# A decoder layer's down projection: from eight column blocks to seven products of halves

## The chip, the cores and the metric

One core of a Trainium2 chip runs the whole layer in one launch. The metric is the device time of one execution in microseconds; smaller is better.

## The reference, cut to what matters

Batch 1, 512 tokens, width 1024, float32. The layer computes `x = x + mixers(norm(x))` and then a gated feed-forward block with a causal depthwise convolution of width 3, and a last norm:

```python
def conv_gated_ffn(h, w_up, conv_w, conv_b, w_down):
    up = causal_depthwise_conv(h @ w_up, conv_w, conv_b)     # 1024 -> 2 x 2816
    gate, val = jnp.split(up, 2, axis=-1)
    return (jax.nn.silu(gate) * val) @ w_down                # 2816 -> 1024

x = x + conv_gated_ffn(rms_norm(x, ffn_norm), w_up, conv_w, conv_b, w_down)
return rms_norm(x, final_norm)
```

The change lies in the last product (512 x 2816 by 2816 x 1024), the residual after it and the last norm.

## The kernel before, in words

**Precision.** Every large product runs in three passes of a reduced float32 type. `split` and `wsplit` (L65 to L77) make a high part by a cast on ACT and a low part by a subtraction on DVE; `mm3` (L79) issues high x high, high x low and low x high into the same PSUM bank.

**Weights.** `wtile` (L56) loads a tile of up to 128 x 1024 from DRAM on SP's queue into one of three raw buffers; `wsplit` writes one of three pairs of high and low buffers. A load waits until the split of the tile three before it has read its buffer, and a split waits until the matmuls three tiles back have read theirs.

**Order.** The code is written stage by stage: input projections, attention and spatial gating, output projection (L563), up projection (L614), down projection (L641), last columns and last norm (L682). The tile framework places waits where buffers and data demand them, and each engine and each queue runs its instructions in order.

**Up stage (L590 to L626).** For each of 22 channel blocks of 128, two weight tiles (gate and value) are multiplied with the normalised activations `hH`, `hL` (8 tiles of 128 x 512 each, width by tokens), 24 matmuls of 512 columns each. `conv` (L599) scales, convolves on ACT and DVE, L623 takes the SiLU, L625 multiplies, and L626 splits the result into `aH[i]`, `aL[i]`: channels by tokens.

**Down stage (L641 to L678).** For six of the eight output blocks of 128 columns, 22 blocks of channels x 3 matmuls accumulate `pd`: width by tokens, weights stationary, 512 tokens moving. Then the residual is added (L649), squared (L651), summed into `acc3` and scaled by the gain. The last two blocks' weights `w_e` are loaded and split once, ahead (L657 to L678), into the buffers of `hH`, `hL`.

**The end (L682 to L735).** The last two column blocks are multiplied for the first 384 tokens (L689), whose norm needs sums over partitions by small matmuls (`rooted`, `over_partitions`) and whose output leaves as width by tokens. The last 128 tokens are done by token: activations stationary, 256 columns of weights moving (L705), the six finished blocks transposed on PE (L693), the mean of squares per partition.

**POOL** does a few powers (the root of the norms), a mask and memsets; it issues no DMA.

Of the kernel before, what the change touches and what calls it, by code (L numbers as in the profile page):

```python
# [42 lines left out]
def block_kernel(ctx, tc, xT, pos, w_s, w_v, w_g, w_q, w_kv, w_o, w_u, w_d,  # L43
                 ws_t, bs, vg, vb, par, cst, w_e, fnl, out, outB):
# [569 lines left out]
    for i in range(NF):  # L614
        pg = up(2 * i)
        if i == 0:
            rt = rooted([acc2], 0, f2, "f")
            pv = up(1)
            A.copy(r2, over_partitions(rt, f2, "f"))
        yg = conv(pg, i)  # L620
        if i:
            pv = up(2 * i + 1)
        A.activation(out=yg, in_=yg, func=AF.Silu)  # L623
        yv = conv(pv, NF + i)
        V.tensor_tensor(out=yv, in0=yg, in1=yv, op=ALU.mult)  # L625
        split(aH[i], aL[i], yv)  # L626

    acc3 = fp.tile([P, S], F32, name="acc3")

    def gain(j):  # L630
        return part[:, PFN + j:PFN + j + 1]

    def dweights(j):
        parts = []
        for lo, hi in ((0, 8), (8, 15), (15, 22)):
            n = (hi - lo) * P
            raw = wtile(w_d[j, :, lo * P:hi * P], f"d{j}{lo}", cols=n)
            parts.append((hi - lo,) + tuple(wsplit(raw, f"d{j}{lo}", 0, n)))
        return parts

    for j in range(KC - 2):  # L641
        pd = bank(f"pd{j}")
        i = 0
        for n, wh, wl in dweights(j):
            for a in range(n):
                c = slice(a * P, (a + 1) * P)
                mm3(pd, wh[:, c], wl[:, c], aH[i], aL[i], i == 0, i == NF - 1)
                i += 1
        V.tensor_tensor(out=x1[j], in0=pd, in1=x1[j], op=ALU.add)  # L649
        sq = acc3 if j == 0 else f2.tile([P, S], F32, tag="z", name=f"sq3_{j}")  # L650
        A.activation(out=sq, in_=x1[j], func=AF.Square)  # L651
        if j:
            V.tensor_tensor(out=acc3, in0=acc3, in1=sq, op=ALU.add)
        A.mul(x1[j], x1[j], gain(j))
        if j == 1:

            eh, el = [], []  # L657
            xh = fp.tile([P, 6 * 2 * P], F32R, name="xh")
            xl = fp.tile([P, 6 * 2 * P], F32R, name="xl")
            for q in range(6):  # L660
                lo = q * 1024
                raw = wtile(w_e[:, lo:min(lo + 1024, NF * 2 * P)], f"e{q}", cols=min(1024, NF * 2 * P - lo))
                for k in range(4):
                    i = 4 * q + k
                    if i >= NF:
                        continue
                    if i < 16:
                        if i % 2 == 0:
                            t = i // 2
                            th = hp.tile([P, S], F32R, tag=f"hH{t}", name=f"eH{t}")  # L670
                            tl = hp.tile([P, S], F32R, tag=f"hL{t}", name=f"eL{t}")
                            split(th, tl, raw[:, k * 256:k * 256 + S])
                        o = (i % 2) * 256
                    else:
                        th, tl, o = xh, xl, (i - 16) * 256
                        split(th[:, o:o + 256], tl[:, o:o + 256], raw[:, k * 256:k * 256 + 256])
                    eh.append(th[:, o:o + 256])
                    el.append(tl[:, o:o + 256])  # L678
# [3 lines left out]
    n = S - P  # L682
    tA, tB = slice(0, n), slice(n, S)
    pA, sqA = None, []
    for j in (KC - 2, KC - 1):
        pA = bank(f"pA{j}")
        for i in range(NF):
            c = slice((j - KC + 2) * P, (j - KC + 3) * P)
            mm3(pA[:, :n], eh[i][:, c], el[i][:, c], aH[i][:, tA], aL[i][:, tA], i == 0, i == NF - 1)  # L689
            if j == KC - 2 and i == 11:  # L690
                pT = [bank("pTa"), bank("pTb")]
                for k in range(KC - 2):
                    T.transpose(pT[k // 4][:, (k % 4) * P:(k % 4 + 1) * P], x1[k][:, tB], ident)  # L693
                pmB = bank("pm_B")
                col_mean(pmB[:, :1], [acc3[:, tB]], 0)
                mB = fp.tile([P, 4], F32, name="mB")
                V.tensor_scalar(out=mB[:, 0:1], in0=pmB[:, 0:1], scalar1=EPS, scalar2=None, op0=ALU.add)
        V.tensor_tensor(out=x1[j][:, tA], in0=pA[:, :n], in1=x1[j][:, tA], op=ALU.add)
        sq = f2.tile([P, n], F32, tag="z", name=f"sqA{j}")
        A.activation(out=sq, in_=x1[j][:, tA], func=AF.Square)  # L700
        V.tensor_tensor(out=acc3[:, tA], in0=acc3[:, tA], in1=sq, op=ALU.add)
        A.mul(x1[j][:, tA], x1[j][:, tA], gain(j))
    pB = bank("pB")
    for i in range(NF):
        mm3(pB[:, :256], aH[i][:, tB], aL[i][:, tB], eh[i], el[i], i == 0, i == NF - 1)  # L705
        if i == 1:

            for k in range(2):
                T.matmul(pB[:, k * P:(k + 1) * P], lhsT=x1[KC - 2 + k][:, tB], rhs=ident, start=False, stop=False)
        if i == 4:  # L710
            rt = rooted([acc3[:, tA]], 0, f2, "A", cols=NT - 1)
        if i == 12:
            pb = over_partitions(rt, f2, "A", cols=NT - 1)
            for q in range(KC // 2):
                for j in (2 * q, 2 * q + 1):
                    V.tensor_tensor(out=x1[j][:, tA], in0=x1[j][:, tA], in1=pb, op=ALU.mult)
                    if q in (0, 3):
                        SY.dma_start(out[j], x1[j][:, tA])
                if q in (0, 3):
                    continue  # L720
                SY.dma_start(out[2 * q:2 * q + 2].rearrange("j p t -> p j t"),
                             x1t[q].rearrange("p (j t) -> p j t", j=2)[:, :, tA])
# [92 lines left out]
```

## Time and profile before

| | us |
|---|---|
| median of 3 runs (708.59 to 710.53) | 708.83 |
| the profiled execution, its own time | 709.26 |
| its span | 707.6 |
| PE busy in it | 699.6 |
| DVE busy | 476.5 |
| ACT busy | 331.5 |
| POOL busy | 12.3 |

PE busy counts the time in which a matmul runs. A matmul's own duration overlaps that of the next one, so the pace is read from starts. "Idle before" of an engine, in brackets or behind the bar, is the time it stood still ahead of an instruction, and what ended that. DMA share is the mean busy share of the core's 16 DMA engines.

### The profile page before, as it was taken

The numbers are of one execution on the slowest core, as the hardware profiler recorded it, in microseconds if no ns is written. First come the engines' busy times: TensorE is split into PE (matmuls) and PEld (weight loads), VectorE is DVE, ScalarE is ACT, GpSimd is POOL, SyncE is SP. The second block draws the span as 40 slices with busy tenths as digits, with TensorE's granted clock in tenths as the row PEclk, the third lists the DMA queues.
The fourth block names the chain that finished last, engine by engine and source line by source line (L and its number), as shares of the span: only waits on it lengthen the run. The fifth ranks groups of instructions, "written<-read, shape, count | busy, mean of one in ns | idle before, by whom it ended". The sixth has DMA issues, their size and how long they took to land.

```text
span 707.6 us, 8629 instructions
## 1 busy us (share of the span) xinstructions
PE 699.6 (99%) x3303; PEld 586.6 (83%) x3303; DVE 476.5 (67%) x817; ACT 331.5 (47%) x496; POOL 12.3 (2%) x16
## 2 busy tenths in 40 slices
PE   9999999999999999999999999999999999999996
PEld 6888888888888888888888888888888888888896
DVE  8875799877777578755587777777677765433104
ACT  5464556676667533433454444444444444423101
POOL 0000110000000000000100000000000000000000
PEclk9999999999999999999999999999999999999999
...
GB/s 260 179 77 135 168 83 82 60 113 40 69 72 60 33 87 76 190 94 105 93 98 89 90 102 107 90 90 100 108 89 91 95 98 163 194 87 48 0 1 120
DMA packets 22617, 69.63 MB, mean 98 GB/s; under 512 B 2736, under 2 KB 4400, under 8 KB 22576
## 3 DMA queue, kind: packets, MB, share of 16 engines
q1 hardware_dynamic: 21568, 66.72, 28.9%
...
q8 instruction: 26, 0.43, 0.3%
...
## 4 chain that ended last, share of the span: by engine, by line
PE 94%; DVE 3%; DMA 2%; issue 0%; ACT 0%; SPq 0%; POOLq 0%; DVEq 0%
PE pup L81 11%; PE pup L82 11%; PE pup L80 11%; PE pd L81 4%; PE pd L80 4%; PE pd L82 4%; PE pout L81 2%; PE pout L80 2%; PE pout L82 2%; PE pzb L82 2%; PE pzb L80 2%; PE pzb L81 2%; PE pv L80 2%; PE pv L82 2%; PE pza L81 2%; PE pv L81 2%
## 5 line engine op out<-in xcount | busy, mean ns | idle before, releaser
L70 ACT CAST wh_u<-wr_u 128x1024 fp32r<-128x1024 f32 x44 | 46.3, 1052 | 41.6 <-PE pup L81 29.5
L71 DVE TENSOR_TENSOR wl_u<-wr_u,wh_u 128x1024 fp32r<-128x1024 f32 x44 | 53.9, 1226 | 8.0 <-ACT wh_u L70 7.0
L604 DVE TENSOR_TENSOR z<-pup,r 128x512 f32<-128x512 f32 x44 | 30.2, 688 | 35.1 <-PE pup L82 35.1
L80 PE MATMUL pd<-aH,wh_d 128*128 128x512 f32 x132 | 51.3, 389 | 0.0
L81 PE MATMUL pd<-aL,wh_d 128*128 128x512 f32 x132 | 51.3, 389 | 0.0
L82 PE MATMUL pd<-aH,wl_d 128*128 128x512 f32 x132 | 51.3, 389 | 0.0
L70 ACT CAST wh_g<-wr_g 128x1024 fp32r<-128x1024 f32 x24 | 25.2, 1050 | 44.4 <-issue 23.3
L76 ACT CAST aH<-y 128x512 fp32r<-128x512 f32 x22 | 13.7, 621 | 56.7 <-DVE z L603 54.2
L71 DVE TENSOR_TENSOR wl_d<-wr_d,wh_d 128x896 fp32r<-128x896 f32 (+1 forms) x18 | 20.5, 1136 | 29.0 <-ACT wh_d L70 28.6
L70 ACT CAST wh_d<-wr_d 128x896 fp32r<-128x896 f32 (+1 forms) x18 | 17.7, 982 | 43.2 <-PE pd L81 35.2
L606 ACT ACTIVATE y<-z,part 128x512 f32<-128x512 f32 x44 | 35.9, 818 | 3.4 <-DVE z L604 1.8
L71 DVE TENSOR_TENSOR wl_g<-wr_g,wh_g 128x1024 fp32r<-128x1024 f32 x24 | 29.4, 1224 | 7.0 <-ACT wh_g L70 6.9
L610 DVE SCALAR_TENSOR_TENSOR y<-z,part,y 128x512 f32<-128x512 f32 x44 | 33.0, 752 | 1.4
L608 DVE SCALAR_TENSOR_TENSOR y<-z,part,y 128x512 f32<-128x512 f32 x44 | 32.8, 747 | 0.3 <-ACT y L606 0.3
L623 ACT ACTIVATE y<-y 128x512 f32<-128x512 f32 x22 | 13.9, 632 | 36.4 <-DVE y L610 36.4
L80 PEld LDWEIGHTS pd<-aH,wh_d 128*128 128x128 f32 x132 | 24.8, 188 | 5.2
L82 PEld LDWEIGHTS pd<-aH,wl_d 128*128 128x128 f32 x132 | 24.8, 188 | 5.2
L81 PEld LDWEIGHTS pd<-aL,wh_d 128*128 128x128 f32 x132 | 24.8, 188 | 5.1
L81 PE MATMUL pout<-mL,wh_o 128*128 128x512 f32 x64 | 25.4, 397 | 0.0
L82 PE MATMUL pout<-mH,wl_o 128*128 128x512 f32 x64 | 25.3, 395 | 0.0
L80 PE MATMUL pout<-mH,wh_o 128*128 128x512 f32 x64 | 25.2, 396 | 0.0
L77 DVE TENSOR_TENSOR aL<-y,aH 128x512 fp32r<-128x512 f32 x22 | 15.2, 693 | 14.2 <-ACT aH L76 14.2
...
## 6 DMA issues: line engine op xcount, KB each, us to landing
wr_u<-in_w_u_dram SPq DMA_DIRECT2D x44, 512.0 KB, 3.3
wr_g<-in_w_g_dram SPq DMA_DIRECT2D x24, 512.0 KB, 3.3
...
wr_v<-in_w_v_dram SPq DMA_DIRECT2D x8, 512.0 KB, 4.2
wr_o<-in_w_o_dram SPq DMA_DIRECT2D x8, 512.0 KB, 3.2
wr_d<-in_w_d_dram SPq DMA_DIRECT2D x6, 512.0 KB, 3.5
wr_e<-in_w_e_dram SPq DMA_DIRECT2D x5, 512.0 KB, 3.7
```

Of the source, the lines that this page charges most:

```text
L70: A.copy(th[:, lo:hi], raw[:, lo:hi])
L71: V.tensor_tensor(out=tl[:, lo:hi], in0=raw[:, lo:hi], in1=th[:, lo:hi].bitcast(F32), op=ALU.subtract)
L76: A.copy(th, src)
L77: V.tensor_tensor(out=tl, in0=src, in1=th.bitcast(F32), op=ALU.subtract)
L80: T.matmul(o, lhsT=wh, rhs=xh, start=start, stop=False)
L81: T.matmul(o, lhsT=wh, rhs=xl, start=False, stop=False)
L82: T.matmul(o, lhsT=wl, rhs=xh, start=False, stop=stop)
L604: V.tensor_tensor(out=z[:, 2:], in0=pz, in1=r2, op=ALU.mult)
L606: A.activation(out=y, in_=z[:, 2:], func=AF.Identity, scale=part[:, w + 2:w + 3], bias=part[:, PCB + f:PCB + f + 1])
L608: V.scalar_tensor_tensor(out=y, in0=z[:, 1:S + 1], scalar=part[:, w + 1:w + 2], in1=y, op0=ALU.mult, op1=ALU.add)
L610: V.scalar_tensor_tensor(out=y, in0=z[:, 0:S], scalar=part[:, w:w + 1], in1=y, op0=ALU.mult, op1=ALU.add)
L623: A.activation(out=yg, in_=yg, func=AF.Silu)
```

## The change

The product is cut into halves in all three directions: tokens 0 to 255 and 256 to 511 (A1x, A2x), channels 0 to 1407 and 1408 to 2815 (Ax1 with B1x, Ax2 with B2x), output columns 0 to 511 and 512 to 1023. Seven products of halves take the place of eight, in Winograd's form, in the order m1, m5, m6, m4, m3, m7, m2:

| product | left | right |
|---|---|---|
| m1 | A11 | B11 |
| m5 | A21 - A22 | B11 + B12 |
| m6 | A21 - A22 - A11 | B11 + B12 + B22 |
| m4 | A22 | B11 + B12 + B21 + B22 |
| m3 | A12 + A21 - A22 - A11 | B22 |
| m7 | A11 - A21 | B12 + B22 |
| m2 | A12 | B21 |

Each product has 2 blocks of 128 tokens (stationary) by 512 columns (moving) over 11 channel blocks, cut into five steps of two blocks and one of one; a step of two is 12 matmuls.

- *Left sides.* The up stage keeps its result unsplit in `aT`, channel blocks of the two halves in turn; after every two blocks of each half `a_sides` splits A11 and forms the four sums in place on DVE. The other six left sides are split during the product before.
- *Right sides.* m1 and m2 read their weights through `wtile` on SP's queue. For the other five, six tiles `R` (which take the memory of `hH`, `hL` of the up stage, now one tile `h0` to `h7` each) are filled from POOL's queue: B11 plain, B12 added; and after each step's split the next change: + B22, + B21, B22 anew, + B12. Adding is done by the DMA (`accum_op`).
- *Residual.* It is transposed to token-major in the up stage (`x1_turn`: 32 transposes on PE, 8 copies on ACT). Parts that several outputs share are added into it by DMAs from POOL's queue (`plus`, 16 of them, 128 KB each); the rest by DVE out of PSUM (`done`).
- *The end.* All tokens are done by token: squares with their sum on ACT, root on POOL, gain and root on DVE and ACT, two stores per 128 tokens (SP and ACT). m2's last three steps run for its first token block, then for its second. `w_e`, the transposes and norm matmuls of the old end are gone; the gain is loaded for the whole width, later.

The diff, without the removed lines of the old down stage and end (they stand above, L614 to L735) and the plumbing of arguments:

```diff
@@ -161,8 +160,8 @@
     hL = [None] * KC
 
     def htiles(j, n):
-        hH[j] = hp.tile([P, S], F32R, tag=f"hH{j}", name=f"hH{j}{n}")
-        hL[j] = hp.tile([P, S], F32R, tag=f"hL{j}", name=f"hL{j}{n}")
+        t = hp.tile([P, D], F32R, tag=f"h{j}", name=f"h{j}{n}")
+        hH[j], hL[j] = t[:, :S], t[:, S:]
...
@@ -557,8 +556,8 @@
             split(mH[h], mL[h], zz)
 
 
-        x1t = [hp.tile([P, D], F32, tag=f"d{t}", name=f"x1_{t}") for t in range(NT)]
-        x1 = [x1t[j // 2][:, (j % 2) * S:(j % 2 + 1) * S] for j in range(KC)]
+        x1t = [hp.tile([P, NT, NT, P], F32, tag=f"d{t}", name=f"x1_{t}") for t in range(2)]
+        x1 = [x1t[j // NT][:, j % NT].rearrange("p t c -> p (t c)") for j in range(KC)]
         acc2 = hp.tile([P, S], F32, name="acc2")
         for j in range(KC):
             SY.dma_start(x1[j], xT[j])
...
@@ -582,10 +581,26 @@
 
 
     fp = ctx.enter_context(tc.tile_pool(name="fp", bufs=1))
-    f2 = ctx.enter_context(tc.tile_pool(name="f2", bufs=2))
     r2 = fp.tile([P, S], F32, name="r2")
-    aH = [fp.tile([P, S], F32R, name=f"aH{i}") for i in range(NF)]
-    aL = [fp.tile([P, S], F32R, name=f"aL{i}") for i in range(NF)]
+    aT = fp.tile([P, NF, S], F32, name="aT")
+    KH = NF // 2
+    S2 = S // 2
+    s1 = fp.tile([P, KH, S2], F32, name="s1")
+    s4 = fp.tile([P, KH, S2], F32, name="s4")
+    a1h = fp.tile([P, KH, S2], F32R, name="a1h")
+    a1l = fp.tile([P, KH, S2], F32R, name="a1l")
+    def a_sides(lo, hi):
+        A11, A21 = aT[:, lo:hi, :S2], aT[:, lo:hi, S2:]
+        A12, A22 = aT[:, KH + lo:KH + hi, :S2], aT[:, KH + lo:KH + hi, S2:]
+        h_, l_, s1_, s4_ = (t[:, lo:hi] for t in (a1h, a1l, s1, s4))
+        split(h_, l_, A11)
+        V.tensor_tensor(out=s1_, in0=A21, in1=A22, op=ALU.subtract)
+        V.tensor_tensor(out=A21, in0=A11, in1=A21, op=ALU.subtract)
+        V.tensor_tensor(out=A11, in0=s1_, in1=A11, op=ALU.subtract)
+        V.tensor_tensor(out=s4_, in0=A12, in1=A11, op=ALU.add)
 
     def up(f):
         raw = wtile(w_u[f], f"u{f}")
@@ -611,128 +626,195 @@
                                op0=ALU.mult, op1=ALU.add)
         return y
 
...
+    def x1_turn(t, hf):
+        pt = bank(f"pt{t}{hf}")
+        for q in range(NT):
+            T.transpose(pt[:, q * P:(q + 1) * P], x1t[hf][:, q, t, :], ident)
+        A.copy(x1t[hf][:, :, t, :], pt.rearrange("p (q c) -> p q c", q=NT))
+    with tc.tile_pool(name="f2", bufs=2) as f2:
+        for n in range(NF):
+            i = n // 2 + (n % 2) * KH
+            pg = up(2 * n)
+            if n == 0:
+                rt = rooted([acc2], 0, f2, "f")
+                pv = up(1)
+                A.copy(r2, over_partitions(rt, f2, "f"))
+            yg = conv(pg, i)
+            if n:
+                pv = up(2 * n + 1)
+            A.activation(out=yg, in_=yg, func=AF.Silu)
+            yv = conv(pv, NF + i)
+            V.tensor_tensor(out=aT[:, i], in0=yg, in1=yv, op=ALU.mult)
+            if n % 4 == 3 or n == NF - 1:
+                a_sides(n // 4 * 2, n // 2 + 1)
+            if 4 <= n < 12:
+                x1_turn((n - 4) // 2, n % 2)
+    dp = ctx.enter_context(tc.tile_pool(name="dp", bufs=1))
+    steps = [(g, min(g + 2, KH)) for g in range(0, KH, 2)]
+    NS = len(steps)
+    blocks = [(0, 4), (4, 8), (8, KH)]
+    B11, B12, B21, B22 = (w_d[k, f] for k in range(2) for f in range(2))
+    ms = fp.tile([P, NT, 4], F32, name="ms")
+    gfb = fp.tile([P, D], F32, name="gfb")
+    A.dma_start(gfb, fnl.to_broadcast([P, D]))
+    R = [hp.tile([P, D], F32, tag=f"h{g}", name=f"r1_{g}") for g in range(NS)]
+    def cols(g):
+        lo, hi = steps[g]
+        return slice(lo * S, hi * S)
+    def fill(t, q, g, add=True):
+        c = cols(g)
+        n = c.stop - c.start
+        if add:
+            G.dma_start(t[g][:, :n], q[:, c], accum_op=ALU.add)
+        else:
+            G.dma_start(t[g][:, :n], q[:, c])
+    left = {
+        "m5": lambda lo, hi: s1[:, lo:hi],
+        "m6": lambda lo, hi: aT[:, lo:hi, :S2],
+        "m4": lambda lo, hi: aT[:, KH + lo:KH + hi, S2:],
+        "m3": lambda lo, hi: s4[:, lo:hi],
+        "m7": lambda lo, hi: aT[:, lo:hi, S2:],
+        "m2": lambda lo, hi: aT[:, KH + lo:KH + hi, :S2],
+    }
+    order = ["m1", "m5", "m6", "m4", "m3", "m7", "m2"]
+    after = {"m5": (B22, True), "m6": (B21, True), "m4": (B22, False), "m3": (B12, True)}
+    parts = {}
+    def a_split(n, b):
+        lo, hi = blocks[b]
+        w = (hi - lo) * S2
+        ah = dp.tile([P, 4 * S2], F32R, tag="ah", name=f"ah_{n}{lo}", bufs=3)
+        al = dp.tile([P, 4 * S2], F32R, tag="al", name=f"al_{n}{lo}", bufs=3)
+        split(ah[:, :w].rearrange("p (k t) -> p k t", t=S2), al[:, :w].rearrange("p (k t) -> p k t", t=S2),
+              left[n](lo, hi))
+        parts[n, b] = (ah, al)
+    def a_of(n, k, m):
+        if n == "m1":
+            return tuple(t[:, k, m * P:(m + 1) * P] for t in (a1h, a1l))
+        c = slice((k % 4) * S2 + m * P, (k % 4) * S2 + (m + 1) * P)
+        return tuple(t[:, c] for t in parts[n, k // 4])
+    ws_ = {}
+    def w_split(n, g):
+        c = cols(g)
+        w = c.stop - c.start
+        if n in ("m1", "m2"):
+            raw = wtile((B11 if n == "m1" else B21)[:, c], f"{n}{g}", cols=w)
+        else:
+            raw = R[g]
+        ws_[n, g] = wsplit(raw, f"{n}{g}", 0, w)
+        if n in after:
+            fill(R, after[n][0], g, after[n][1])
+    def res(t, f):
+        return x1t[f][:, :, t, :]
+    def b3(t):
+        return t.rearrange("p (q c) -> p q c", q=NT)
+    def plus(t, f, t_):
+        for q in (slice(0, 2), slice(2, 4)):
+            G.dma_start(res(t, f)[:, q], b3(t_)[:, q], accum_op=ALU.add)
+    def done(t, f, p_, op=ALU.add):
+        V.tensor_tensor(out=res(t, f), in0=res(t, f), in1=b3(p_), op=op)
+        j_ = dp.tile([P, S], F32, tag="j", name=f"j{t}{f}", bufs=2)
+        A.activation(out=b3(j_), in_=res(t, f), func=AF.Square, accum_out=ms[:, t, f:f + 1])
+        if f:
+            V.tensor_tensor(out=res(t, f), in0=res(t, f), in1=b3(gfb[:, S:]), op=ALU.mult)
+    def finish(t):
+        V.tensor_scalar(out=ms[:, t, 2:3], in0=ms[:, t, 0:1], scalar1=ms[:, t, 1:2], scalar2=1.0 / D,
+                        op0=ALU.add, op1=ALU.mult)
+        V.tensor_scalar(out=ms[:, t, 2:3], in0=ms[:, t, 2:3], scalar1=EPS, scalar2=None, op0=ALU.add)
+        G.tensor_tensor(out=ms[:, t, 3:4], in0=ms[:, t, 2:3], in1=mhalf[:, 0:1], op=ALU.pow)
+        r_ = ms[:, t, 3:4]
+        V.scalar_tensor_tensor(out=res(t, 0), in0=res(t, 0), scalar=r_, in1=b3(gfb[:, :S]),
+                               op0=ALU.mult, op1=ALU.mult)
+        A.mul(res(t, 1), res(t, 1), r_)
+        SY.dma_start(out[t, :, :S], res(t, 0))
+        A.dma_start(out[t, :, S:], res(t, 1))
+    p1, p5 = ([fp.tile([P, S], F32, name=f"{n}{m}") for m in range(2)] for n in ("p1", "p5"))
+    def post(n, b, ms_=(0, 1)):
+        for m in ms_:
+            if n == "m1":
+                A.copy(p1[m], b[m])
+                plus(m, 0, p1[m])
+            if n == "m5":
+                A.copy(p5[m], b[m])
+            if n == "m6":
+                V.tensor_tensor(out=p1[m], in0=b[m], in1=p1[m], op=ALU.add)
+                V.tensor_tensor(out=p5[m], in0=p5[m], in1=p1[m], op=ALU.subtract)
+                plus(m, 1, p5[m])
+                plus(2 + m, 1, p5[m])
+            if n == "m4":
+                V.tensor_tensor(out=p1[m], in0=b[m], in1=p1[m], op=ALU.add)
+                plus(2 + m, 0, p1[m])
+            if n == "m3":
+                done(m, 1, b[m])
+            if n == "m7":
+                done(2 + m, 0, b[m])
+                done(2 + m, 1, b[m], ALU.subtract)
+                finish(2 + m)
+            if n == "m2":
+                with tc.high_priority():
+                    done(m, 0, b[m])
+                    finish(m)
+    seq = [(n, g) for n in order for g in range(NS)]
+    turn_ = {}
+    for i, n in enumerate(order[1:], 1):
+        for b in range(3):
+            turn_.setdefault(b if i == 1 else NS * (i - 1) + (4, 6, 8)[b], []).append((n, b))
+    for g in range(2):
+        w_split(*seq[g])
+    for g in range(NS):
+        fill(R, B11, g, False)
+    for g in range(NS):
+        fill(R, B12, g)
+    acc_ = None
+    def steps_of(n, g, ms_):
+        wh, wl = ws_[n, g]
+        lo, hi = steps[g]
+        for k in range(lo, hi):
+            cw = slice((k - lo) * S, (k - lo + 1) * S)
+            for m in ms_:
+                ah, al = a_of(n, k, m)
+                mm3(acc_[m], ah, al, wh[:, cw], wl[:, cw], k == 0, k == KH - 1)
+    for i, (n, g) in enumerate(seq):
+        if i + 2 < len(seq):
+            w_split(*seq[i + 2])
+        for x in turn_.get(i, ()):
+            a_split(*x)
+        if g == 0:
+            acc_ = [bank(f"{n}_{m}") for m in range(2)]
+        if n != order[-1] or g < NS - 3:
+            steps_of(n, g, (0, 1))
+            if g == NS - 1:
+                post(n, acc_)
+    for m in range(2):
+        for g in range(NS - 3, NS):
+            steps_of(order[-1], g, (m,))
+        post(order[-1], acc_, (m,))
 def _layout(x, positions, mix_norm, w_in, a_v_norm_g, a_v_norm_b, a_spatial_w, a_spatial_b, q_a_norm,
...
     up = cols(w_up[0])
-    a["w_u"] = c(np.stack([up[:NF], up[NF:]], axis=1).reshape(2 * NF, P, D))
-    a["w_d"] = c(cols(w_down[0][:, :D - 2 * P]))
-    a["w_e"] = c(w_down[0][:, D - 2 * P:].reshape(NF, P, 2 * P).transpose(1, 0, 2).reshape(P, NF * 2 * P))
-    a["fnl"] = c(final_norm[D - 2 * P:].reshape(1, 2 * P))
+    up = np.stack([up[:NF], up[NF:]], axis=1).reshape(2, NF // 2, 2, P, D)
+    a["w_u"] = c(up.transpose(1, 0, 2, 3, 4).reshape(2 * NF, P, D))
+    a["w_d"] = c(w_down[0].reshape(2, NF // 2, P, 2, S).transpose(0, 3, 2, 1, 4).reshape(2, 2, P, -1))
```

## Rows read from the trace of the kernel before

**Rows 1.** The page, part 1: engine, busy us, share of the span, instructions.

```profile
PE 699.6 (99%) x3303; PEld 586.6 (83%) x3303; DVE 476.5 (67%) x817; ACT 331.5 (47%) x496; POOL 12.3 (2%) x16
```

**Rows 2.** The page, part 4: the chain that ended last, by engine.

```profile
PE 94%; DVE 3%; DMA 2%; issue 0%; ACT 0%; SPq 0%; POOLq 0%; DVEq 0%
```

**Rows 3.** Timeline of PE, matmuls: start us, us, engine, line, operation.

```profile
578.10 0.39 PE L80 MATMUL pd<-aH,wh_d 128*128 128x512 f32 x1
...
649.73 0.39 PE L81 MATMUL pd<-aL,wh_d 128*128 128x512 f32 x1
...
661.97 0.39 PE L81 MATMUL pd<-aL,wh_d 128*128 128x512 f32 x1
...
674.13 0.60 PE L693 MATMUL pTa<-cstt,x 128*128 128x128 f32 x4
674.56 0.38 PE L693 MATMUL pTb<-cstt,x 128*128 128x128 f32 x2
...
689.05 0.33 PE L80 MATMUL pA<-aH,xh 128*128 128x384 f32 x1
...
691.48 0.33 PE L82 MATMUL pA<-aH,xl 128*128 128x384 f32 x1
...
694.91 0.28 PE L80 MATMUL pB<-eH,aH 128*128 128x256 f32 x1
...
696.71 0.28 PE L80 MATMUL pB<-eH,aH 128*128 128x256 f32 x1
```

**Rows 4.** Chain that ended last, in order of time: start us, us, what.

```profile
701.05 0.13 PE pB L82
```

**Rows 5.** Timeline of the end, ACT, DVE and SP's queue.

```profile
701.21 0.38 ACT L726 ACTIVATE oB<-pB 128x256 f32<-128x256 f32 x1 [4.45 <-PE pB L82]
...
701.72 0.42 DVE L727 TENSOR_TENSOR xB<-pB,gfb 128x256 f32<-128x256 f32 x1 [0.40 <-ACT oB L726]
...
703.07 0.69 ACT L731 ACTIVATE oB<-pTa,mB 128x512 f32<-128x512 f32 x1 [1.38 <-POOL mB L730]
...
703.96 0.33 SPq L735 DMA_DIRECT2D out_dram<-oB  x1
```

**Rows 6.** Groups of DVE by form, from 340 us: xcount, busy us, mean ns.

```profile
L610 DVE SCALAR_TENSOR_TENSOR y<-z,part,y 128x512 f32<-128x512 f32 x44 | 33.0, 752 | 1.4
...
L71 DVE TENSOR_TENSOR wl_d<-wr_d,wh_d 128x1024 fp32r<-128x1024 f32 x6 | 7.4, 1225 | 14.1 <-ACT wh_d L70 14.1
...
L649 DVE TENSOR_TENSOR x<-pd,x 128x512 f32<-128x512 f32 x6 | 4.1, 691 | 22.9 <-PE pd L82 22.9
```

**Rows 7.** Groups of ACT by form, from 340 us: the same columns.

```profile
L70 ACT CAST wh_d<-wr_d 128x1024 fp32r<-128x1024 f32 x6 | 6.3, 1054 | 11.6 <-PE pd L81 8.9 <-DMA wr_d<-in_w_d_dram 1.7 <-PE pup L81 1.0
...
L651 ACT ACTIVATE sq<-x 128x512 f32<-128x512 f32 x5 | 3.2, 632 | 14.1 <-DVE x L649 14.1
```

**Rows 8.** Windows: length, busy of PE, PEld, DVE, ACT, POOL; clock, DMA share, GB/s.

```profile
345.00:577.00 232.00, 232.00 (x1025) 192.06 (x1025) 171.26 (x260) 107.35 (x134) 0.94 (x1) 1.00 0.30 96
577.00:670.00 93.00, 93.00 (x415) 77.37 (x414) 35.75 (x46) 31.41 (x44) 0.00 (x0) 1.00 0.33 100
...
0.00:17.70 17.70, 16.28 (x62) 10.98 (x63) 14.36 (x32) 10.34 (x18) 1.24 (x6) 1.00 0.82 260
```

**Rows 9.** DMA: a queue's packets, MB, share; issues xcount, KB, us to landing.

```profile
q1 hardware_dynamic: 21568, 66.72, 28.9%
...
wr_u<-in_w_u_dram SPq DMA_DIRECT2D x44, 512.0 KB, 3.3
...
bsb<-in_bs_dram ACTq DMA_DIRECT2D x1, 512.0 KB, 8.2
```

**Rows 10.** Groups of POOL by form, whole span: xcount, busy us, mean ns.

```profile
L148 POOL TENSOR_TENSOR rt_f<-ms_f,mhalf 128x4 f32<-128x4 f32 x1 | 1.9, 1856 | 226.7 <-DVE ms_f L147 226.7
```

**Rows 11.** Timeline of ACT in the up stage.

```profile
480.20 1.05 ACT L70 CAST wh_u<-wr_u 128x1024 fp32r<-128x1024 f32 x1 [1.01 <-PE pup L81]
```

More of the change, by code (lines that the diff above doesn't have):

```diff
@@ L43, in block_kernel @@
 def block_kernel(ctx, tc, xT, pos, w_s, w_v, w_g, w_q, w_kv, w_o, w_u, w_d,
-                 ws_t, bs, vg, vb, par, cst, w_e, fnl, out, outB):
+                 ws_t, bs, vg, vb, par, cst, fnl, out):
     nc = tc.nc
@@ L86, in block_kernel @@
     gx = cp.tile([P, KC], F32, name="gx")
-    gfb = cp.tile([P, 2 * P], F32, name="gfb")
     cstt = cp.tile([P, NCST], F32, name="cstt")
@@ L178, in block_kernel @@
     ckL = mx.tile([P, S], F32R, name="ckL")
-    vA = [hp.tile([P, D], F32, tag=f"d{t}", name=f"vA{t}") for t in range(NT)]
+    vA2 = [hp.tile([P, 2 * D], F32, tag=f"d{t}", name=f"vA{t}") for t in range(2)]
+    vA = [vA2[t // 2][:, (t % 2) * D:(t % 2 + 1) * D] for t in range(NT)]
     with tc.tile_pool(name="st", bufs=2) as st:
@@ L612, in conv @@
         return y
[L614 to L678, printed above, removed]
@@ L682, in block_kernel @@
[L682 to L722, printed above, removed]
@@ L723, in block_kernel @@
-    oB = fp.tile([P, D], F32, name="oB")
-    xB = fp.tile([P, 2 * P], F32, name="xB")
-    with tc.high_priority():
-        A.activation(out=oB[:, S + 256:], in_=pB[:, :256], func=AF.Square, accum_out=mB[:, 1:2])
-        V.tensor_tensor(out=xB, in0=pB[:, :256], in1=gfb, op=ALU.mult)
-        V.tensor_scalar(out=mB[:, 2:3], in0=mB[:, 1:2], scalar1=1.0 / D, scalar2=mB[:, 0:1],
-                        op0=ALU.mult, op1=ALU.add)
-        G.tensor_tensor(out=mB[:, 3:4], in0=mB[:, 2:3], in1=mhalf[:, 0:1], op=ALU.pow)
-        A.mul(oB[:, :S], pT[0], mB[:, 3:4])
-        V.tensor_scalar(out=oB[:, S:S + 256], in0=pT[1][:, :256], scalar1=mB[:, 3:4], scalar2=None, op0=ALU.mult)
-        V.tensor_scalar(out=oB[:, S + 256:], in0=xB, scalar1=mB[:, 3:4], scalar2=None, op0=ALU.mult)
-        A.dma_start(outB[:, :S], oB[:, :S])
-        SY.dma_start(outB[:, S:], oB[:, S:])
+    def x1_turn(t, hf):
[3 more added lines that the diff above has]
+        A.copy(x1t[hf][:, :, t, :], pt.rearrange("p (q c) -> p q c", q=NT))
@@ L807 @@
                                    kind="ExternalInput").ap())
-    args.append(nc.dram_tensor("out_0_dram", (KC, P, S - P), F32, kind="ExternalOutput").ap())
-    args.append(nc.dram_tensor("out_1_dram", (P, D), F32, kind="ExternalOutput").ap())
+    args.append(nc.dram_tensor("out_0_dram", (NT, P, D), F32, kind="ExternalOutput").ap())
     with tile.TileContext(nc) as tc:
@@ L812 @@
     r = run_bass_kernel_spmd(nc, [maps], core_ids=[0])
-    a, b = (np.asarray(r.results[0][f"out_{i}_dram"]) for i in range(2))
-    return np.ascontiguousarray(np.concatenate([a.reshape(D, S - P).T, b]))[None]
+    return np.ascontiguousarray(np.asarray(r.results[0]["out_0_dram"]).reshape(S, D))[None]
```

4 lines of the change are left out of this document (2 added, 2 removed).

## The prediction

> **What bounds the kernel now.** I read the busy table first: PE is busy for 699.6 of 707.6 us, POOL for 12.3 [rows 1]. The chain that ended last agrees: 94% of it is PE [rows 2], so time comes off only where PE gets fewer or shorter matmuls. Then the matmul timeline gives the pace [rows 3], because a matmul's duration (0.39 us) overlaps the next one's. From 649.73 to 661.97 us lie 54 steps of 512 columns, 0.2267 us each; from 689.05 to 691.48 lie 14 of 384 columns, 0.174 each; from 694.91 to 696.71 lie 15 of 256 columns, 0.120 each. The down projection starts at 578.10 us, called T below [rows 3], and its last matmul ends at 701.18 [rows 4]: 123.1 us, with PE never idle in the window 577 to 670 and the granted clock 1.00 [rows 8]. In that window DVE works 35.8 and ACT 31.4 of 93 us: there is room on both.
>
> The profiled execution took 709.26 us (span 707.6 plus 1.7 around it), 0.43 above the median of 708.83. I sum against 709.26 and take 0.4 off at the end.
>
> **What it removes on PE.** Before: 6 column blocks x 22 x 3 = 396 matmuls of 512 columns, 132 of 384 and 66 of 256; 396 x 0.2267 + 132 x 0.174 + 66 x 0.120 = 89.8 + 23.0 + 7.9 = 120.7 us; transposes and the norms' small matmuls fill the 123.1. After: seven products, each 11 x 2 x 3 = 66 matmuls of 512 columns: 462 x 0.2267 = 104.7 us, and the norms and the token-major tail need no matmul. Gain 18.4 us. One product lasts 15.0 us, a step of 12 matmuls 2.72.
>
> **What it adds on PE.** 32 transposes in the up stage. Four took from 674.13 to 674.56, 0.11 each [rows 3]: +3.5 us, on the path, as PE has no idle time to give.
>
> **The tail.** Today 1.86 us pass from the square on ACT (701.21) to the last scaling (703.07) [rows 5]. After, a PSUM add of 0.69 (L649 [rows 6]) precedes it; the square is 512 columns wide, 0.63 (L651 [rows 7]) for 0.38, and one more small DVE operation follows; against it the product with the gain leaves the chain (0.42, L727 [rows 5]). I take +0.6 us. The last scaling, 0.75 on DVE (L610's kind [rows 6]) beside 0.69 on ACT, and two 256 KB stores are as now. The other half of m2's tokens, and all of m7's, finish under later matmuls; without that cover each would cost this tail again, some 7 us.
>
> **ACT and DVE in the down stage.** Weight splits grow from 22 to 38.5 tiles of 1024 columns, 1.05 us on ACT and 1.23 on DVE each [rows 6, 7]. Per product: DVE 5.5 x 1.23 + 5.5 x 0.69 for the left side = 10.5 us, ACT 5.5 x 1.05 + 5.5 x 0.63 = 9.2 us, of 15.0. Nothing on the path, as long as splits aren't held up by their source.
>
> **The up stage.** For each four channel blocks, four 512-column subtractions become five (one split, four sums), 0.69 us more per pair of pairs, under 4 us for the stage; DVE has 61 of 232 us free there [rows 8]. The reordered blocks cost nothing; eight ACT copies of some 0.63 us [rows 7] lie in ACT's free half [rows 8]. m1 reads only the first half of the channels and half of the tokens, and its last block is wanted 13.6 us after T, so the last convolution stays hidden as it is today.
>
> **The new queue: adding DMAs on POOL.** Six tiles R hold the weights' sums, in the memory of the up stage's left operands: the first is free 21 matmuls before T (T-4.8). Each product changes R in place: 6 loads of B11, 6 adds of B12, then after each split the next fill (three rounds of adds in all later, one of plain loads), and 16 adds of 128 KB into the residual. POOL issues 52 DMAs where it issued none; SP issues 12 weight loads for 24 and four stores for seven, ACT the gain's load and four stores, 0.33 us each [rows 5], off the path. Each fill waits for a split, each split of the next product (R + 2.5 us of cast and subtraction) waits for the fill, and behind a waiting cast on ACT stand the next left-side splits: PE starves if fills are late.
>
> A plain transfer: the SP queue's packets took 28.9% of the span for 66.72 MB, 326 GB/s with all engines busy, so 1.61 us of the engines for 512 KB, of 3.3 to landing [rows 9]. Up to the last fill that m7 needs the engines carry, in tiles of 512 KB: plain 5.5 (B11) + 2.5 (m1's weights beyond the three raw buffers, which are filled ahead) + 5.5 (B22) + 3 (m2's first three buffers) + 1 (the gain) = 17.5, or 28.2 us; adding 4 x 5.5 + 16 x 0.25 = 26, or 41.8 us times f, the price of an adding byte in plain ones. The window runs from T-3.1 (4.8 before T, 1.7 until the bytes flow) to T + 5 x 15.0 + 13.6 - 2.5 = T+86: 89 us. What is above that, PE waits for.
>
> No row shows an adding DMA. Below, f = 1: it moves at least the bytes of a load. Above, f = 2.5: the 512 KB load into bsb took 8.2 us against 3.3 [rows 9]. I take 1.5, a read and a write becoming two reads and a write, nearer the plain load, whose shape and source the fills have: 28.2 + 62.7 = 90.9, so PE waits 1.9 us. At the start of m5, R's first tile is behind 8 plain ones: T - 3.1 + 12.9 + 1.6f = T+12.2, wanted at T+12.5: no wait.
>
> The Trainium skill speaks against this price: Collectives: The Full Stack, The bandwidth ceiling: the fold count and why AG ≠ RS ≠ AR, says that a DMA that adds is slower because both operands are read on the same side, 62.28 against 32.35 GB/s, a ratio of 1.93. By it the sum would be 28.2 + 80.7 = 108.9, 19.9 us of waiting and 714.5 us; no run here shows it yet.
>
> **Sum.** -18.4 + 3.5 + 0.6 = -14.3, so 695.0; +1.9 of waiting is 696.9; against the median 696.5.
>
> **Rivals.**
> 1. *Adding costs two plain transfers* (slower). The destination is read as the source is, one after the other, f = 2: 28.2 + 83.6 = 111.8, 22.8 us over the window, 717.3 us. It decides from f = 1.80 on, where the waits eat all 14.3. For it: the window is short, 4 x 2.9 MB of adding in 75 us. Against it: 326 GB/s comes from loads with pauses between them; the kernel's first 17.7 us moved 260 GB/s on average at a share of 0.82 [rows 8], so no stretch shows the engines' ceiling. At 400 GB/s f = 2 gives only 91 us. The chances below count f in plain transfers at 326.
> 2. *POOL is the limit.* An issue costs SP 0.33 us (L735 [rows 5]); POOL's dearest row is 1.86 us [rows 10]. 52 x 0.33 = 17 us hides; 52 x 1.86 = 97 us against 91 (T-4.8 to T+86) adds 6, 701 us. Beyond 2 us each the gain is gone; at 2.5 it is 130, +39, 734 us.
> 3. *The DMAs are entirely hidden* (f up to 1.45): 694.6 us.
> 4. *The change doesn't do what it says*: the halves' matmuls run slower than 0.2267 us, or the bursts of five sums delay a weight split in the up stage. Each split is ready two matmul groups ahead (a cast starts at 480.20 us, as the group that freed its buffer ends [rows 11], with the next group's weights already split), so a burst of 3.5 us fits; for 14.3 us to go, 462 matmuls would need 0.258 each, and no 512-column row has that pace.
>
> **How the numbers follow.** A measurement here can tell about 0.3%, 2.1 us, from no change. f under 1.75 (rival 3 with 0.27, the forecast's region up to 1.75 with 0.30) is faster: 0.57. f from 1.75 to 1.85: 0.06, same. f above 1.85: 0.29; POOL beyond 2.1 us each: 0.05; rival 4 or a stall I don't see: 0.03; together slower: 0.37. Range: the low end is f = 1 with tail and transposes 2 us cheaper, 692.5; the high end is f = 2.1 (116 us, +27), 722. That leaves out about 0.03 below and 0.15 above. As both signs hold much, the forecast's own range is 692.5 to 701.
>
> **What would show it.** Right: 462 matmuls of 512 columns at 0.2267 us, the down stage some 107 us long, fills of 512 KB landing well within 12 us of issue, ACT's casts of R waiting on DMA for no more than 2 us in sum, a tail near 7 us. The dear addition would show as casts of m5, m6, m4 and m7 each waiting on an adding DMA, with the engines' share near 1 from T on and PE idle between steps. A limit on POOL would show as the same waits with the DMA engines' share well below 1. I am wrong if the up stage grows by more than 4 us, or if PE's pace falls.

## The result and the profile after

The change makes the kernel slower: 743.75 us median (743.22 to 745.29, 4 runs) against 709.0 (708.59 to 710.53, 4 runs) of the kernel before, a ratio of 1.049 (95% interval [1.0477, 1.0503]; below, brackets behind a ratio are that interval). The forecast was 696.5, in a range of 692.5 to 701.

The page after, span and busy times as in [rows 1]:

```profile
span 742.4 us, 8528 instructions
...
PE 699.6 (94%) x3183; PEld 573.9 (77%) x3183; DVE 518.6 (70%) x851; ACT 353.0 (48%) x518; POOL 60.9 (8%) x70
```

PE is now idle for 6% of the span, and its busy time is no smaller, although it runs 120 matmuls fewer. In the next lines of the page, 40 slices of 18.6 us each with the busy share and PE's granted clock in tenths, both losses, idle time and a lower clock, are seen from the 34th slice (612 us) on:

```profile
PE   8999999999999999999999999999999996972795
...
PEclk9999999999999999999999999999999997895988
DMA  8425322130211123523322322232323897946644
```

The chain that ended last, by engine, answers to [rows 2]: PE had 94% of it.

```profile
PE 78%; issue 8%; DMA 6%; POOL 4%; DVE 2%; ACT 1%; SPq 0%; POOLq 0%; ACTq 0%; DVEq 0%
```

"issue" at 8% is the new thing: time in which an engine stood still and the profile shows nothing that it waited for. The groups of POOL from 560 us on say which engine and which instructions (xcount, busy us, mean ns, then the idle time before them and what ended it):

```profile
L675 POOL DMA_DIRECT2D r<-in_w_d_dram x24 | 22.8, 975 | 36.3 <-issue 23.6 <-DVE wl_m L71 7.8 <-DMA wr_m<-in_w_d_dram 2.6
L729 POOL DMA_DIRECT2D x<-p x16 | 19.2, 1198 | 41.9 <-issue 31.9 <-DVE wl_m L71 3.8 <-DVE al_m L77 3.2
L677 POOL DMA_DIRECT2D r<-in_w_d_dram x12 | 7.5, 712 | 234.2 <-ACT wh_m L70 232.1 <-DVE wl_m L71 1.1 <-issue 0.6
```

These are the 24 adding fills, the 16 additions into the residual and the 12 plain fills, 52 DMAs. POOL itself is busy with them for 49.5 us, but stands for 56.1 us more (23.6 + 31.9 + 0.6) before them without a visible reason. Such idle time, ended by "issue", is called a hold below. The timeline of POOL shows the worst stretch (start us, busy us, instruction, in brackets the idle time before it):

```profile
645.22 0.82 POOL L677 DMA_DIRECT2D r<-in_w_d_dram  x1
647.12 0.55 POOL L677 DMA_DIRECT2D r<-in_w_d_dram  x1 [1.08 <-DVE wl_m L71]
650.92 1.24 POOL L729 DMA_DIRECT2D x<-p  x1 [3.24 <-DVE al_m L77]
654.41 1.20 POOL L729 DMA_DIRECT2D x<-p  x1 [2.25 <-issue]
...
675.31 1.20 POOL L729 DMA_DIRECT2D x<-p  x1 [2.27 <-issue]
676.04 2.14 POOL L677 DMA_DIRECT2D r<-in_w_d_dram  x3
678.78 0.55 POOL L677 DMA_DIRECT2D r<-in_w_d_dram  x1 [0.61 <-issue]
```

After m6, eight additions of 128 KB leave one every 3.48 us, (675.31 - 650.92) / 7. The median time from issue to landing of such an addition is 3.2 us, so each leaves about when the one ahead has landed. In the program the second of a pair (654.41) waits on no semaphore. Behind the eight, in POOL's order, stand the plain fills of m3's third to sixth weight tiles, which leave from 676.04 on. ACT's cast needs them, and PE the cast. Timelines of ACT and PE:

```profile
681.30 1.04 ACT L70 CAST wh_m<-r 128x1024 fp32r<-128x1024 f32 x1 [22.56 <-DMA r<-in_w_d_dram]
```

```profile
663.30 0.40 PE L82 MATMUL m<-wh_m,al_m 128*128 128x512 f32 x1
682.40 0.79 PE L80 MATMUL m<-wh_m,ah_m 128*128 128x512 f32 x1 [18.70 <-ACT wh_m L70]
683.66 0.79 PE L81 MATMUL m<-wl_m,ah_m 128*128 128x512 f32 x1 [0.47 <-DVE wl_m L71]
684.25 0.63 PE L82 MATMUL m<-wh_m,al_m 128*128 128x512 f32 x1
684.67 0.63 PE L80 MATMUL m<-wh_m,ah_m 128*128 128x512 f32 x1
```

PE stands still for 18.7 us before m3's third step. In this wait the DMA engines are not the limit. Windows (length, busy of PE, PEld, DVE, ACT, POOL; granted clock, DMA share, GB/s):

```profile
580.00:600.00 20.00, 20.00 (x90) 16.50 (x89) 13.93 (x19) 10.45 (x13) 6.33 (x9) 1.00 1.04 313
...
660.00:680.00 20.00, 3.70 (x16) 2.63 (x14) 0.00 (x0) 0.00 (x0) 8.83 (x10) 0.66 0.42 57
...
682.40:686.60 4.20, 3.73 (x8) 2.65 (x9) 4.20 (x4) 2.94 (x3) 1.21 (x1) 0.50 1.03 249
```

From 660 to 680 their share is 0.42, at 57 GB/s, and DVE and ACT are wholly idle, so neither of them keeps POOL from handing over the additions. The third row shows a second price: behind the gap the granted clock is 0.50, the 1.2 GHz level, and a matmul takes 0.427 us from start to start (684.25 to 684.67) for 0.233.

**Where the 47 us against the forecast lie.** Starts of the 462 matmuls: the down stage runs from 582.45 to 734.44 us, 152.0, where the forecast had 106.6 (104.7 + 1.9). Against 0.2267 us for each matmul, seventeen intervals above half a microsecond hold 37.7 us more; the longest, 18.9, is the one above, the next ones are 4.2 (m7), 3.6 and 2.1 (m6). Thirty-eight intervals from 0.3 to 0.5 us, most of them at the low clock, cost 7.1 us, and a pace of 0.2333 for 0.2267 us in m5 to m2 another 2.3 (m1 alone keeps 0.2267). The up stage and what lies before it give 0.9, the tail 1.0 more than forecast.

### The profile page after: what moved, and what is told of

Its sections match the earlier page's. It is cut to its first block, busy times and chain, and to the rows that moved or that the text cites. A ratio compares the mean times of both kernels' runs of the same rounds, so it can differ in the third digit from the quotient of the medians.

```text
span 742.4 us, 8528 instructions
## 1 busy us (share of the span) xinstructions
PE 699.6 (94%) x3183; PEld 573.9 (77%) x3183; DVE 518.6 (70%) x851; ACT 353.0 (48%) x518; POOL 60.9 (8%) x70
## 4 chain that ended last, share of the span: by engine, by line
PE 78%; issue 8%; DMA 6%; POOL 4%; DVE 2%; ACT 1%; SPq 0%; POOLq 0%; ACTq 0%; DVEq 0%
PE pup L80 11%; PE pup L82 11%; PE pup L81 11%; DMA r<-in_w_d_dram 5%; POOL x L729 2%; PE pout L81 2%; PE pout L80 2%; PE pout L82 2%; PE pv L80 2%; PE pzu L82 2%; PE pzb L82 2%; PE pzb L80 2%; PE pzu L81 2%; PE pzb L81 2%; PE pza L82 2%
## 5 line engine op out<-in xcount | busy, mean ns | idle before, releaser
L80 PE MATMUL m<-wh_m,ah_m 128*128 128x512 f32 x132 | 56.0, 424 | 27.9 <-ACT wh_m L70 27.9
L71 DVE TENSOR_TENSOR wl_m<-r,wh_m 128x1024 fp32r<-128x1024 f32 (+1 forms) x30 | 33.8, 1134 | 57.4 <-ACT wh_m L70 57.2
L70 ACT CAST wh_m<-r 128x1024 fp32r<-128x1024 f32 (+1 forms) x30 | 29.3, 977 | 67.9 <-DMA r<-in_w_d_dram 62.0
L81 PE MATMUL m<-wl_m,ah_m 128*128 128x512 f32 x132 | 56.4, 428 | 4.2 <-DVE wl_m L71 4.1
L82 PE MATMUL m<-wh_m,al_m 128*128 128x512 f32 x132 | 55.3, 419 | 0.3 <-DVE al_m L77 0.3
L80 PEld LDWEIGHTS m<-wh_m,ah_m 128*128 128x128 f32 x132 | 26.8, 203 | 36.8 <-ACT wh_m L70 30.5
L81 PEld LDWEIGHTS m<-wl_m,ah_m 128*128 128x128 f32 x132 | 26.7, 202 | 13.8 <-DVE wl_m L71 7.5
L82 PEld LDWEIGHTS m<-wh_m,al_m 128*128 128x128 f32 x132 | 26.8, 203 | 6.9 <-DVE al_m L77 0.7
L677 POOL DMA_DIRECT2D r<-in_w_d_dram x12 | 7.5, 712 | 234.2 <-ACT wh_m L70 232.1
L675 POOL DMA_DIRECT2D r<-in_w_d_dram x24 | 22.8, 975 | 36.3 <-issue 23.6
```

Source lines behind the costliest of these rows:

```text
L70: A.copy(th[:, lo:hi], raw[:, lo:hi])
L71: V.tensor_tensor(out=tl[:, lo:hi], in0=raw[:, lo:hi], in1=th[:, lo:hi].bitcast(F32), op=ALU.subtract)
L80: T.matmul(o, lhsT=wh, rhs=xh, start=start, stop=False)
L81: T.matmul(o, lhsT=wh, rhs=xl, start=False, stop=False)
L82: T.matmul(o, lhsT=wl, rhs=xh, start=False, stop=stop)
L675: G.dma_start(t[g][:, :n], q[:, c], accum_op=ALU.add)
```

## The experiments

**The theories.** Theory A: POOL can't hand a DMA over before there is room for its descriptors (the entries that describe its rows), one per row; with the room of this program (1024) an addition of 256 rows of 512 bytes fills it, so additions go one at a time, and whatever stands behind them on POOL waits. Rivals: adding costs the engines so much that the fills are late (rival 1 of the prediction); POOL's own work at each issue is the limit (rival 2); the additions are slow by their bytes, not by their rows. Each kernel below is the changed one with the edit shown. The kernel before took 708.71 to 709.81 us beside these runs, so times of different sections can be compared to about 1 us.

**More room, nothing else.**

```diff
-    nc = bacc.Bacc("TRN2", target_bir_lowering=False, num_devices=1, dynamic_dma_scratch_size=1024)
+    nc = bacc.Bacc("TRN2", target_bir_lowering=False, num_devices=1, dynamic_dma_scratch_size=2048)
```

> The changed kernel with twice the room for POOL's DMA descriptors (scratch size 2048 in place of 1024), nothing else. Theory A (POOL holds each adding DMA back until earlier ones have left the descriptor room: eight additions of 128 KB left at a pace of 3.49 us with the engines' share at 0.37 from 650 to 676 us): their pace falls to about POOL's own 1.2 us, the additions of 512 KB leave earlier, the PE gap at 660 to 680 us shrinks by 12 us or more; 715 to 728 us. Theory B (adding itself is dear: 190 to 205 GB/s with the engines' share at 1.0 from 628 to 646 us): more room changes nothing that counts, 739 to 745 us.

710.42 us (709.01 to 712.23), 1.0018 [1.0006, 1.0031] of the kernel before. The time lies below the 715 to 728 expected: this one number gives back 33 of the 35 us, with the same DMAs, bytes and instructions. POOL in the same stretch:

```profile
637.59 1.20 POOL L729 DMA_DIRECT2D x<-p  x1 [0.63 <-issue]
641.44 1.17 POOL L729 DMA_DIRECT2D x<-p  x1 [2.64 <-issue]
644.55 6.03 POOL L729 DMA_DIRECT2D x<-p  x5 [1.94 <-issue]
649.94 2.84 POOL L677 DMA_DIRECT2D r<-in_w_d_dram  x4
```

Five of the eight now leave back to back, 1.2 us each, POOL's own time. But holds of 10.2 us are left before the additions, and PE still loses 2.5 us at m3's third step, with the low clock behind it (0.57 from 656 to 664 us).

**The additions into the residual on DVE.** Room as in the change.

```diff
-        for q in (slice(0, 2), slice(2, 4)):
-            G.dma_start(res(t, f)[:, q], b3(t_)[:, q], accum_op=ALU.add)
+        V.tensor_tensor(out=res(t, f), in0=res(t, f), in1=b3(t_), op=ALU.add)
```

> The 16 additions of 128 KB into the residual are taken off POOL's queue and made by 8 additions of 512 columns on DVE, 0.69 us each; room stays 1024. Theory A or its sister C (the fills of R stand behind those additions on POOL's queue): 16 x 3.5 us leave POOL's queue, at least the 27 us from 650 to 676; 708 to 720 us. Theory B: only 2 MB of adding traffic out of 13.6 leave, 735 to 742 us.

702.52 us (701.78 to 703.0), 0.9905 [0.9887, 0.9924]: 41 us less than the change, by eight DVE operations in place of 16 DMAs, and below the 708 to 720 expected. The adding fills are still held, 26.1 us in 12 places, but this lies beside PE's work: PE loses 2.7 us. So what mattered was not that POOL stood, but what stood behind it.

**Both.** More room and the additions on DVE.

> Room 2048 and the residual's additions on DVE together. Theory A with C: only the engines' own price of the 24 adding fills is left, 5.5 x 2.7 = 14.9 us a product against PE's 15.0: 699 to 707 us, with small waits at m5's start. Theory B: 730 us or more.

701.83 us (701.6 to 704.42), 0.9901 [0.9879, 0.9924], the same as the one before within what can be told. POOL's holds at the fills are down to 0.2 us. Without them, the price of adding can be read, because the fills now follow on each other: the DMA engines from 606 to 616 us (total, then the share of POOL's queue).

```profile
DMA packets 648, 2.11 MB, mean 211 GB/s; under 512 B 70, under 2 KB 70, under 8 KB 648
...
q0 software_dynamic: 646, 2.10, 107.3%
```

**The same with plain loads.** The weights' sums are left out: the 24 adding fills overwrite the tile in place of adding to it.

```diff
         if add:
-            G.dma_start(t[g][:, :n], q[:, c], accum_op=ALU.add)
+            G.dma_start(t[g][:, :n], q[:, c])
```

> As the run with both, and the 24 adding fills of R are plain loads of the same bytes (the sums of the weights are left out). What this run gains over the one with both is the price of adding on the DMA engines. Theory A with C: at most 8 us, 695 to 699 us in all. Theory B: 25 us or more, to the same 695 to 699 us, the time that PE's matmuls alone would give.

699.59 us (699.28 to 700.91), 0.9865 [0.9847, 0.9883], just above the 695 to 699 expected. The engines, full with plain fills of the same queue, from 583 to 588 us:

```profile
DMA packets 575, 2.07 MB, mean 414 GB/s; under 512 B 69, under 2 KB 69, under 8 KB 574
...
q0 software_dynamic: 551, 2.02, 99.8%
```

An adding byte costs 414 / 211 = 1.96 plain ones. What that is worth is 701.83 - 699.59 = 2.2 us, and the down stages of the two profiles agree: 109.95 us from the first start to the last against 107.67. The waits are at m5's second to fourth steps, 2.3 us; they are gone with plain loads.

**Fewer rows, the same bytes.** The room is 1024 again and all additions are DMAs, but the residual is laid out so that the 512 columns of a token stand together: 8 additions of 256 KB in 128 rows of 2 KB, for 16 of 128 KB in 256 rows of 512 bytes.

```diff
-        return x1t[f][:, :, t, :]
+        return x1t[f][:, t]
...
-        for q in (slice(0, 2), slice(2, 4)):
-            G.dma_start(res(t, f)[:, q], b3(t_)[:, q], accum_op=ALU.add)
+        G.dma_start(res(t, f).rearrange("p q c -> p (q c)"), t_, accum_op=ALU.add)
```

> The changed kernel with room 1024 and all additions by DMA, but the residual's tiles laid out with each token block's 512 columns in one run: the additions into it become 8 DMAs of 256 KB with 128 rows of 2 KB in place of 16 of 128 KB with 256 rows of 512 bytes. The same bytes, a quarter of the rows. Theory A (what holds POOL is the room for descriptors, one per row): several of these fit at once, the 3.49 us pace between them goes, 706 to 722 us. Rival D (each adding DMA into a tile waits until the one before it into the same tile has landed, whatever its rows): 8 waits of 3 to 4 us in place of 16, 725 to 735 us. If bytes alone count: 740 us or more.

706.04 us (705.62 to 708.01), 0.9952 [0.9935, 0.9969]. POOL after m6:

```profile
641.94 0.88 POOL L732 DMA_DIRECT2D x<-p  x1 [1.91 <-DVE wl_m L71]
643.51 0.86 POOL L732 DMA_DIRECT2D x<-p  x1 [0.69 <-issue]
644.80 0.86 POOL L732 DMA_DIRECT2D x<-p  x1 [0.42 <-DVE wl_m L71]
647.28 0.85 POOL L732 DMA_DIRECT2D x<-p  x1 [1.62 <-issue]
647.87 2.52 POOL L681 DMA_DIRECT2D r<-in_w_d_dram  x4
```

The same megabyte is handed over from 641.94 to 648.13 where the change took from 650.92 to 676.51. With bytes and room unchanged and a quarter of the rows, 38 us are back: the rows set the hold, not the bytes, as theory A has it. How much room a row takes, theory A had wrong. Counted from the issue and the landing of each DMA, at most 384 rows of adding DMAs were under way at once with room 1024 (the changed kernel, the additions on DVE, this run) and up to 896 with 2048, but 768 rows of plain ones with 1024 (the first six fills). So one addition of 256 rows does not fill the room, but a second does not go beside it, and an adding row takes more of it than a plain one. The holds before the adding fills stay, 27.8 us, and PE still loses some 7 us.

**Fewer rows and more room.**

> The residual laid out in runs of 512 columns, with room 2048, all additions still by DMA. Theory A: the additions into the residual cost only their bytes, 2 MB at some 200 GB/s, partly hidden: 702 to 708 us, 2 to 8 below the run with more room alone. Rival D: no better than 709 us.

703.11 us (702.51 to 703.81), 0.9902 [0.9882, 0.9922]. The group of the eight additions names no "issue" any more (0.2 us of it are left):

```profile
L732 POOL DMA_DIRECT2D x<-p x8 | 7.2, 976 | 3.2 <-DMA wr_m<-in_w_d_dram 2.0 <-DVE p L765 0.5 <-DMA r<-in_w_d_dram 0.3
```

So adding by DMA and adding on DVE come out alike once POOL is not held.

**The pace of the matmuls.** What was left was 0.2333 us per matmul in m5 to m2 where m1 and the kernel before [rows 3] have 0.2267. PE in the run with both remedies, 72 steps in 16.80 us:

```profile
640.12 0.39 PE L80 MATMUL m<-wh_m,ah_m 128*128 128x512 f32 x1
...
656.92 0.39 PE L80 MATMUL m<-wh_m,ah_m 128*128 128x512 f32 x1
```

First try: the kernel with both remedies and one small tile widened, which shifts all that follows it by 64 bytes.

```diff
-    ms = fp.tile([P, NT, 4], F32, name="ms")
+    ms = fp.tile([P, NT, 8], F32, name="ms")
```

> The run with both repairs, and one small tile (ms) is 64 bytes larger, so that every tile allocated behind it, the split left sides among them, starts 64 bytes later; no instruction changes. The matmuls of m1 run at 0.2267 us each and those of m5 to m2 at 0.2333, and the only difference seen is where their stationary side lies. If its place relative to 128 bytes sets the pace: 396 x 0.0066 = 2.6 us less, 698.5 to 700 us, all matmuls at 0.2267. If it is something else, such as how far up in the memory it lies: no change, 701 to 703 us.

701.05 us (700.91 to 701.23), 0.9873 [0.9854, 0.9892], and the pace goes from 0.2333 to 0.2324, a seventh of the way to 0.2267: the place within 128 bytes matters a little and is not the main cause. Second try, from that kernel: the split left sides of m5 to m2 move from bytes 199 to 223 thousand of each partition down to 94 to 119 thousand. m1's thereby rise to 189 to 211 thousand, and four small groups (`ms`, `gfb`, `p1`, `p5`) to the top.

```diff
+    lp = ctx.enter_context(tc.tile_pool(name="lp", bufs=1))
     fp = ctx.enter_context(tc.tile_pool(name="fp", bufs=1))
...
-        ah = dp.tile([P, 4 * S2], F32R, tag="ah", name=f"ah_{n}{lo}", bufs=3)
-        al = dp.tile([P, 4 * S2], F32R, tag="al", name=f"al_{n}{lo}", bufs=3)
+        ah = lp.tile([P, 4 * S2], F32R, tag="ah", name=f"ah_{n}{lo}", bufs=3)
+        al = lp.tile([P, 4 * S2], F32R, tag="al", name=f"al_{n}{lo}", bufs=3)
```

> The padded kernel with the split left sides of m5 to m2 (ah, al) moved from the top of the memory (byte 200 thousand and above of each partition) to byte 94 thousand, and m1's left side (a1h, a1l) thereby moved up to 188 and 200 thousand; nothing else changes. If the height at which the stationary tiles lie sets the pace of the matmuls, the products m5 to m2 go from 0.2324 to 0.2267 us each and m1 from 0.2267 to 0.2324 or part of the way: 396 x 0.0057 = 2.3 us less, 66 x 0.0057 = 0.4 us more, 699.1 us against 701.05. If the height is not the cause (the shorter tiles of four blocks, or what else runs beside m5 to m2), the paces stay at 0.2267 for m1 and 0.2324 for the others, and the time within 0.5 us of 701.05.

Timelines of PE in the middle of the down stage, first without the move, then with it:

```profile
639.84 0.39 PE L80 MATMUL m<-wh_m,ah_m 128*128 128x512 f32 x1
...
657.27 0.39 PE L80 MATMUL m<-wh_m,ah_m 128*128 128x512 f32 x1
```

```profile
639.69 0.39 PE L80 MATMUL m<-wh_m,ah_m 128*128 128x512 f32 x1
...
657.37 0.39 PE L80 MATMUL m<-wh_m,ah_m 128*128 128x512 f32 x1
```

75 steps in 17.43 us are 0.2324 each; 78 in 17.68 are 0.2267. So the move restores the pace. m1, moved up, keeps 0.2267, against what was expected, so height alone is no rule; which neighbours matter, or where the border lies, stays open. The time misses its number: 700.92 us (700.09 to 701.86), 0.9888 [0.9871, 0.9904], not the 699.1 expected. The waits at m5's steps grow from 2.4 to 3.4 us, and the down stage shrinks only from 109.7 to 109.1. The move did more than was meant: the gain's load of 512 KB, which left at 340.30 us without it, now leaves among the fills:

```profile
586.27 0.33 ACTq L665 DMA_DIRECT2D gfb<-in_fnl_dram  x1
```

m5's second adding fill lands 17.25 us after the first matmul of m1, for 16.05 without the move. That this load makes up the whole miss is not shown.

**All together.** From the padded kernel, also: the residual laid out as above, and m1's last three weight tiles split from the filled `R` instead of being loaded a second time (2.5 tiles less in the stretch where the engines are full).

```diff
-        if n in ("m1", "m2"):
+        if n == "m2" or (n == "m1" and g < 3):
...
+        if n == "m1" and g >= 3:
+            fill(R, B12, g)
...
-    for g in range(NS):
+    for g in range(3):
         fill(R, B12, g)
```

> A version meant to beat both kernels: additions into the residual on DVE, room 2048, the 64 bytes, the residual in runs of 512 columns (stores of 2 KB rows), the last three steps of m1 split from R (2.5 tiles fewer to load before m5), and the first token block's last scaling issued behind the second one's addition on DVE. If the waits at m5's start (2.0 us), the pace (2.6) and the tail (0.5 to 1) all go: 695.5 to 698 us. If the start of m5 is held by POOL's order rather than by bytes: 697 to 700.

700.23 us (699.75 to 703.75), 0.9871 [0.9848, 0.9893], just above both ranges expected. The three waits in m5 are gone, and one of 1.25 us in m1 has come in their place. A reordering of the last scalings that was to free DVE for the last addition had no effect: DVE still scaled the first token block at 690.28 and added the second at 690.95. With the left sides moved down as well:

> The same move in the version with all the other parts together (700.23 us). Height is the cause: 698.3 us. It is not: 700.2, within 0.5.

697.97 us (697.62 to 699.06), 0.9848 [0.9833, 0.9863]: as expected (698.3), and the fastest kernel of this study, 1.5% below the one before. Waits of 1.0 us in m5 and 0.9 in m2 are left, and the down stage is 106.5 us long.

## Why the prediction was wrong

**The step that failed** is "POOL issues 52 DMAs where it issued none; ... 0.33 us each [rows 5], off the path". It took an issue for a short instruction and laid it off the path. Measured, POOL's own time is 0.55 us for a plain fill, 0.86 for an adding one and 1.2 for an addition of 256 rows, and above all it is held until there is room for the rows: the 52 DMAs took POOL from 578.51 to 705.70 us, 127.2 or 2.45 each, of which 49.5 us are its own work and 56.1 are holds. The prediction names what is queued behind a waiting cast on ACT, but not what is queued on POOL: it says nothing of the order of the eight additions of m6 and the plain fills of m3 behind them. That order turned the holds into 18.7 us of idle PE. In the sum it is the term of PE's waiting, 1.9 us, that came out near 45: 37.7 in long intervals and 7.1 in those at the low clock and other short ones.

**Rival 2**, given 0.05, stood at the right place. Its sum, 52 issues against a window of 91 us, gives 734 us at 2.5 each, where the run took 743.75 at 2.45. Its sign in the profile, waits of casts with the engines' share well below 1, is the one that came: ACT waited 62.0 us for these fills, at a share of 0.42 in the longest wait (around m6, from 628 to 646 us, it was 1.04; what full engines and what late issues cost there is not separated). Its price was wrong in kind: it reckoned POOL's busy time per issue, which more room does not change, and the run with more room is 33 us faster.

**Rival 1 and the price of adding.** In the prediction's unit, plain transfers at 326 GB/s, 211 GB/s are f = 1.55; 1.5 was taken. The ratio of two that rival 1 feared is true (1.96), but so is the argument raised against it, that 326 GB/s is not the ceiling: plain fills reach 414. The waits for it were put at 1.9 us and measured 2.2. They fell at m5's second to fourth steps, though, and not over the whole window; the prediction looked at m5's first tile alone and found no wait. So the nearness of the two figures is partly luck.

The Trainium skill, Collectives: The Full Stack, The bandwidth ceiling: the fold count and why AG ≠ RS ≠ AR, gives 62.28 GB/s for a collective that copies (AllGather) against 32.35 for one that adds (ReduceScatter), 1.93; the traces here, of loads into one core, agree with 1.96. The 714.5 us drawn from it set that ratio on 326 GB/s, and so overrated it.

**The gain on PE** holds where the left sides lie low: with the best version 461 intervals at 0.2267 make 104.5 of its 106.5 us. In the changed kernel a matmul of m5 to m2 took 0.2333, and a fall of the pace is something that the prediction had listed as proof against it; it costs 2.3 us and is not the main cause of the loss.

**The up stage** grew from 240.8 to 244.7 us (337.74 to 582.45 after), 3.9 where 3.5 was forecast for the transposes; the further cost of the sums did hide.

**The tail** took 8.0 us from the last matmul's end (734.44) to the end of the span, 6.4 before [rows 4]: 1.6 more where 0.6 was forecast. Three rows of its timeline show half a microsecond of it:

```profile
734.22 0.75 DVE L745 SCALAR_TENSOR_TENSOR x<-x,ms,gfb 128x512 f32<-128x512 f32 x1 [0.65 <-POOL ms L743]
734.88 0.68 DVE L732 TENSOR_TENSOR x<-x,m 128x512 f32<-128x512 f32 x1
...
738.16 0.47 ACTq L749 DMA_DIRECT2D out_dram<-x  x1
```

The last addition, ready at 734.44, waits for DVE to scale the other token block first. The last store then needs 4.3 us to the end of the span; before it was 3.6 (from 703.96 [rows 5]).

**Cover.** DVE and ACT have the room they were said to have: with the holds gone, in the best version, PE waits for a left side from DVE at one place, 0.9 us in m2; the wait of 1.0 us in m5 ends with DVE's split too, but behind a fill that lands late.
